# An encoder layer with routed experts: the scatter as 0/1 matrices on gate-scaled rows in two f32r parts, and its steps set between the weight chunks

## The chip, the cores and the metric

One core of a Trainium2 chip runs the kernel. The metric is device time in microseconds (us), median of the runs; 1230.35 us for the kernel before (three runs, 1230.09 to 1231.81).

## The reference, cut to what matters

One layer over 512 tokens of width 1024, all float32: a mixing sub-layer (latent attention beside a convolution), and then a routed mixture of 16 experts, which the change concerns. Each expert takes its best 64 tokens, and its result is scaled by the router's gate and added back to those tokens.

```python
def expert_choice_moe(h, w_router, w_gate, w_up, w_down):
    capacity = CAPACITY_FACTOR * S // N_EXPERTS            # 2 * 512 / 16 = 64
    affinity = jax.nn.softmax(logits, axis=-1)             # logits = h @ w_router
    gates, idx = lax.top_k(affinity.transpose(0, 2, 1), capacity)
    xg = jax.vmap(lambda hb, ib: hb[ib])(h, idx)           # 16 x 64 rows
    a = jnp.einsum('becd,edf->becf', xg, w_gate)           # 1024 -> 2048
    u = jnp.einsum('becd,edf->becf', xg, w_up)
    y = jnp.einsum('becf,efd->becd', jax.nn.silu(a) * u, w_down)
    y = y * gates[..., None].astype(y.dtype)
    return ...                                             # zeros.at[idx].add(y)
# then h = layer_norm(DEEPNORM_ALPHA * h + moe, ln2_g, ln2_b)
```

The weights of one expert are three matrices of 8 MB.

## The kernel before, in words

The mixing sub-layer takes the first 274 us or so and is the same in both kernels. It leaves the normalised tokens in `h1`, the affinities in `aff`, and the rank of every token for experts 0 and 1 in `pos`. Then a loop over the 16 experts follows, written out in Python.

**Weights.** An expert's weights are 24 chunks of 1 MB: 8 of w_gate (k = 0), 8 of w_up (k = 1), 8 of w_down. After the first 22 they come two at a time, 2048 KB to a DMA, into a ring of ten big tiles (`stream`, `take_big`, tile b, L157), all from SP's queue. A DMA into a tile waits until TensorE (PE) has read the tile's former chunks. One tile leaves the ring in expert 1 for the accumulator `acc`, another is lent out in expert 3 for the residual (`residual_pieces`).

**One expert on PE.** For each chunk of gate and up, four matmuls, 128x64 weights by 512 columns, go to the two-bank tiles `gu0` and `gu1` (L1140). The two column halves (partitions 0 to 63 and 64 to 127 of the output) run side by side. Silu on ScalarE (ACT) and a product on VectorE (DVE, L1164) give tile sq; eight transposes (L1185, tile tr) and two copies turn it; then 32 matmuls with w_down go to bank `py` (L1214). Every float32 matmul is two instructions in the trace, so L1140 has 128 and L1214 has 64 instructions an expert.

**Gather.** For a pair of experts (2p, 2p+1) `gather` builds a 0/1 matrix `oh` from the ranks (L1036), multiplies it with `h1` in 32 float32 matmuls (L1044, bank sg), and ACT evacuates to xg (L1045). Then GpSimd (POOL) makes a copy of `oh` with the affinities in place of the ones (`gate`, L1053), PE transposes it (L1056), and ACT writes it to a quarter tile q (L1058). This is the scatter matrix of one expert, with the gates in it.

**Scatter.** ACT copies py to a quarter tile (L1222). In the next expert, eight float32 matmuls (four token blocks t by two halves hf of the width; L1066) multiply the scatter matrix with those rows; hf = 0 uses partitions 0 to 63 and hf = 1 partitions 64 to 127. Each result fills one of two sg banks, and DVE adds it to `acc` (L1072).

**Ranks.** For expert e + 2, within expert e: four transposes (L238, tile tr), comparisons on DVE (L240), and small counting matmuls (L245).

**Order.** The program is written in one order, and a scheduler of the framework then places each instruction on its engine's queue by its own estimate of times. What stands on a queue runs in that order. At the end, `norm_rows` normalises `acc` on DVE and POOL (L1101 to L1106) with gains that ACT spreads from PE transposes (L1013, L1014), and the last expert's own rows are normalised straight from py (L1228 to L1240).

Of the kernel before, what the change touches and what calls it, by code (L numbers as in the profile page):

```python
# [46 lines left out]
def layer_kernel(ctx, tc, x, positions, emb_ln_g, emb_ln_b, w_in, q_norm_g, w_qb, kv_norm_g, w_kvb,  # L47
# [62 lines left out]
    def quarter_tile(q):  # L110
        return slots.tile([128, S], F32, name=f"q{q}")
# [140 lines left out]
    def mask_tile(pool):  # L252
        return pool.tile([128, TT, 128], BF16, name="mask", bufs=4)
# [776 lines left out]
    def gather(pair):  # L1030
        oh = wk.tile([128, TT, 2 * CAP], F32, name="oh", bufs=1)
        xg = wk.tile([128, DC, 2 * CAP], F32, name="xg", bufs=1)
        oh4 = oh.rearrange("p t (e s) -> p t e s", e=2)
        pb = pos[:, :, 2 * pair:2 * pair + 2, None].to_broadcast([128, TT, 2, CAP])
        ib = iota[:, None, None, :].to_broadcast([128, TT, 2, CAP])
        nc.vector.tensor_tensor(oh4, ib, pb, op=OP.is_equal)  # L1036
        width = 1 if pair == 0 else 4
        for c0 in range(0, DC, width):
            p = ps.tile([128, 512], F32, name="sg", bufs=2)
            for c in range(width):  # L1040
                cc = c0 + c
                for t in range(TT):
                    rows = h1[:, t, cc // 2 * 256:cc // 2 * 256 + 256].rearrange("p (n a) -> p a n", a=2)[:, cc % 2]
                    nc.tensor.matmul(p[:, c * 128:(c + 1) * 128], rows, oh[:, t, :], start=t == 0, stop=t == TT - 1)  # L1044
                nc.scalar.activation(xg[:, cc, :], p[:, c * 128:(c + 1) * 128], AF.Identity,  # L1045
                                     scale=gbp[:, 0, cc:cc + 1], bias=gbp[:, 1, cc:cc + 1])
            yield xg

        hot[pair] = oh
        for s in range(1 if pair == E // 2 - 1 else 2):  # L1050
            gate = wk.tile([128, TT, 2, CAP], F32, name="gate", bufs=1)
            ab = aff[:, :, 2 * pair + s, None, None].to_broadcast([128, TT, 2, CAP])
            nc.gpsimd.tensor_tensor(gate, oh4[:, :, s, None, :].to_broadcast([128, TT, 2, CAP]), ab, op=OP.mult)  # L1053
            p = ps.tile([128, 512], F32, name="sg", bufs=2)
            for t in range(TT):
                nc.tensor.transpose(p[:, t * 128:(t + 1) * 128], gate[:, t].rearrange("p a s -> p (a s)"), ident)  # L1056
            g = quarter_tile(s)
            nc.scalar.activation(g, p, AF.Identity)  # L1058
            yield g

    def scatter(y, g, e):
        for t in range(TT):
            pp = []
            for hf in range(2):
                p = ps.tile([128, 512], F32, name="sg", bufs=2)
# [43 lines left out]
    hot = {}  # L1109
    residual = None  # L1110
    pend = None
    nxt = gather(0)
    gT = None
    for e in range(E):
        s = e % 2
        if s == 0:
            if e:
                xg, gT, gate_gen = nxt
        pgu = [ps.tile([128, 2, 512], F32, name=f"gu{k}") for k in range(2)]
        if e:  # L1120
            order = [(k, c) for k in range(2) for c in range(DC)]
        else:

            order = [(k, 2 * j + a) for j in range(DC // 2) for k in range(2) for a in range(2)]
        for k, c in order:
            p = pgu[k]
            if e == 0 and k == 0:
                xg = next(nxt)
            if k == 0 and c == 4 and e + 2 < E:
                pr = ps.tile([128, 512], F32, name="tr")  # L1130
                for t in range(TT):
                    m = mask_tile(wk)
                    compare(e + 2, t, pr[:, t % 2 * 128:(t % 2 + 1) * 128], m)
                    count(t, pr[:, 256:256 + TT], m)
                rank(e + 2, pr[:, 256:256 + TT])
            i = 24 * e + 8 * k + c
            w = w_tiles.pop(i)
            for b in range(2):
                for g in range(2):
                    nc.tensor.matmul(p[g * 64:(g + 1) * 64, b, :], xg[:, c, s * CAP:(s + 1) * CAP], w[2 * b + g],  # L1140
                                     start=c == 0, stop=c == DC - 1)
            if residual is not None and k == 1:
                next(residual, None)
            if c % 2 and not LATE <= i < LATE + 2:

                if (e, k, c) == (1, 1, DC - 1):
                    t4 = take_big(back=False)
                    acc.extend(t4[:, t * D:(t + 1) * D] for t in range(TT))
                elif (e, k, c) == (3, 0, 1):
                    residual = residual_pieces()  # L1150
                    next(residual)
                else:
                    stream(next_chunk[0] + 2)
        sg = pair_tile(F32)
        nc.scalar.activation(sg, pgu[0], AF.Silu)  # L1155
        hh = sg
        last = e == E - 1
        if last:
            gate = last_rows()
        for b in range(2):  # L1160
            if last:
                nc.vector.scalar_tensor_tensor(hh[:, b], sg[:, b], gate, pgu[1][:, b], op0=OP.mult, op1=OP.mult)
            else:
                nc.vector.tensor_tensor(hh[:, b], sg[:, b], pgu[1][:, b], op=OP.mult)  # L1164
        if pend is not None:
            scatter(*pend)
# [7 lines left out]
        if s == 1 and e + 1 < E:  # L1174
            gate_gen = gather((e + 1) // 2)
            for _ in range(DC // 4):
                xg_next = next(gate_gen)
            nxt = xg_next, next(gate_gen), gate_gen
        elif e and not last:
            gT1 = next(gate_gen, None)  # L1180
# [9 lines left out]
        if last:  # L1190
# [16 lines left out]
            nc.scalar.activation(warm, eps2, AF.Sqrt)  # L1207
        for c in range(8):
# [66 lines left out]
```

## Time and profile before

| | us |
|---|---|
| median of 3 runs | 1230.35 |
| the profiled execution | 1228.7 |
| its span, first to last instruction | 1226.9 |
| PE busy | 1147.4 (94%) |
| DVE busy | 409.3 (33%) |
| ACT busy | 237.1 (19%) |
| POOL busy | 213.7 (17%) |

The mean granted clock of TensorE was 0.989. Of the span the chain that ended last gives 81% to PE. Weights are 402.7 MB of the 419.6 MB that are read. A time in the rows below is in us from the span's start; "x16" counts instructions that the view merged; "[0.78 <-DVE b L1072]" is idle time before the first of them, and what ended it.

### The profile page before, as it was taken

To read this page: it belongs to the slowest core of one execution; us is meant where nothing else is said; L and a number is where in the kernel's file an instruction comes from. 1 tells how busy PE (TensorE), PEld (TensorE's weight loads), DVE (VectorE), ACT (ScalarE), POOL (GpSimd) and SP (SyncE) were. 2 spreads that over 40 slices of the span, in tenths; PEclk is the share of its full clock that TensorE was granted. 3 is DMA by queue.
4 is the path that set the end of the run, shared out by engine and by line. 5 is a ranking of instruction groups with operands and counts; after the bars stand their busy time and mean duration, and the time that the engine had idled before them with its cause. 6 is when DMAs were issued, how large, how long until landed. Compare 5 with 4: busy or idle time off the path is not lost.

```text
span 1226.9 us, 13587 instructions
## 1 busy us (share of the span) xinstructions
PE 1147.4 (94%) x5553; PEld 536.4 (44%) x5553; DVE 409.3 (33%) x923; ACT 237.1 (19%) x432; POOL 213.7 (17%) x233
## 2 busy tenths in 40 slices
PE   5898998999999999999999899989999998999996
PEld 4687776774334333432433243324333433344332
DVE  6799898451021116212121202020212021101253
ACT  5445687231111000100100010001000100010020
POOL 6778476210000016000000000000000000000031
PEclk9899999999999999999999999999999999999999
DMA  6430016777999899999999999999999999999981
GB/s 198 131 90 33 1 70 203 279 275 303 406 429 411 369 429 377 430 384 427 427 428 428 428 427 427 427 428 427 427 429 428 427 428 428 428 426 428 428 338 77
DMA packets 43680, 422.84 MB, mean 345 GB/s; under 512 B 5178, under 2 KB 13187, under 8 KB 18018
## 3 DMA queue, kind: packets, MB, share of 16 engines
q1 hardware_dynamic: 42032, 421.28, 83.1%
q8 instruction: 43, 0.70, 0.2%
q10 hardware_dynamic: 1506, 0.43, 0.2%
q0 software_dynamic: 80, 0.26, 0.1%
q14 instruction: 19, 0.16, 0.0%
HBM read 419.60 MB, written 2.36 MB: 344 GB/s over the span
## 4 chain that ended last, share of the span: by engine, by line
PE 81%; DVE 7%; DMA 4%; ACT 3%; issue 3%; POOL 2%; POOLq 0%; SPq 0%; ACTq 0%; DVEq 0%
PE gu L1140 34%; PE py L1214 18%; PE sg L1066 6%; PE sg L1044 6%; PE pj L258 3%; PE pj L259 3%; PE pj L260 3%; PE tr L1185 1%; DVE cv L451 1%; DVE b L1072 1%; DVE mask L240 1%; PE st L773 1%; DMA b<-in_w_down_dram 1%; DMA s<-in_w_in_dram 1%; ACT s L227 1%
## 5 line engine op out<-in xcount | busy, mean ns | idle before, releaser
L1140 PE MATMUL gu<-b,xg 128*64 128x512 f32 x1920 | 436.6, 596 | 0.0
L1140 PEld LDWEIGHTS gu<-b,xg 128*64 128x64 f32 x1920 | 138.9, 137 | 259.3 <-issue 250.7
L1214 PE MATMUL py<-b,sq 128*64 128x512 f32 x976 | 228.3, 609 | 0.0
L1072 DVE TENSOR_TENSOR b<-sg,b 128x512 f32<-128x512 f32 x112 | 73.8, 687 | 201.9 <-PE sg L1066 201.3
L1053 POOL TENSOR_TENSOR gate<-oh,aff 128x512 f32<-128x512 f32 x15 | 16.2, 1077 | 683.3 <-DVE oh L1036 315.7
L1214 PEld LDWEIGHTS py<-b,sq 128*64 128x64 f32 x976 | 66.9, 139 | 122.5 <-issue 117.7
L1066 PE MATMUL sg<-q,q 64*128 64x512 f32 x240 | 88.7, 641 | 16.2 <-DVE b L1072 12.2
L1164 DVE TENSOR_TENSOR sq<-sq,gu 128x512 f32<-128x512 f32 x30 | 19.3, 684 | 231.5 <-PE gu L1140 231.5
L258 PE MATMUL pj<-s,s 128*128 128x512 f32 x189 | 77.8, 420 | 7.6 <-ACT q L433 3.2
L240 DVE SCALAR_TENSOR_TENSOR mask<-tr,aff,ones_b 128x128 bf16<-128x128 f32 x84 | 26.1, 348 | 166.0 <-PE tr L238 166.0
L1044 PEld LDWEIGHTS sg<-oh,h 128*128 128x128 f32 x512 | 64.0, 197 | 31.9 <-issue 24.2
L259 PE MATMUL pj<-s,s 128*128 128x512 f32 x189 | 76.8, 406 | 0.0
L1044 PE MATMUL sg<-oh,h 128*128 128x128 f32 x512 | 71.6, 289 | 3.1 <-ACT xg L1045 2.8
L1045 ACT ACTIVATE xg<-sg,gbp 128x128 f32<-128x128 f32 x64 | 28.7, 457 | 217.4 <-PE sg L1044 124.2
L228 POOL TENSOR_TENSOR s<-s,s 128x512 fp32r<-128x512 f32 (+2 forms) x54 | 64.4, 1216 | 19.6 <-ACT s L227 12.8
L451 DVE SCALAR_TENSOR_TENSOR cv<-s,cw,cv 128x512 f32<-128x512 f32 x83 | 62.2, 750 | 1.7
L260 PE MATMUL pj<-s,s 128*128 128x512 f32 x157 | 62.7, 403 | 0.0
L1066 PEld LDWEIGHTS sg<-q,q 64*128 64x128 f32 x240 | 24.1, 184 | 74.9 <-issue 32.5
L1155 ACT ACTIVATE sq<-gu 128x1024 f32<-128x1024 f32 x16 | 16.4, 1023 | 171.3 <-PE gu L1140 171.3
L1222 ACT ACTIVATE q<-py 128x512 f32<-128x512 f32 x15 | 9.0, 597 | 196.3 <-PE py L1214 196.3
L258 PEld LDWEIGHTS pj<-s,s 128*128 128x128 f32 x189 | 37.4, 199 | 16.8 <-ACT q L433 3.7
L240 DVE SCALAR_TENSOR_TENSOR mask<-tr,aff,before 128x128 bf16<-128x128 f32 x56 | 19.4, 347 | 62.8 <-PE tr L238 62.8
(278 smaller groups left out, 1070.2 us busy)
## 6 DMA issues: line engine op xcount, KB each, us to landing
b<-in_w_down_dram SPq DMA_DIRECT2D x60, 2048.0 KB, 13.6
b<-in_w_gate_dram SPq DMA_DIRECT2D x60, 2048.0 KB, 15.3
b<-in_w_up_dram SPq DMA_DIRECT2D x60, 2048.0 KB, 13.7
s<-in_w_gate_dram SPq DMA_DIRECT2D x8, 1024.0 KB, 6.8
s<-in_w_in_dram SPq DMA_DIRECT2D x12, 512.0 KB, 5.1
s<-in_w_up_dram SPq DMA_DIRECT2D x6, 1024.0 KB, 7.2
s<-in_w_down_dram SPq DMA_DIRECT2D x6, 1024.0 KB, 10.9
s<-in_w_o_dram SPq DMA_DIRECT2D x4, 1024.0 KB, 7.0
```

The lines of the kernel that those rows point to most:

```text
L228: pin(eng, eng.tensor_tensor(lo, src, hi.bitcast(F32), op=OP.subtract))
L240: vector(nc.vector.scalar_tensor_tensor(mask[:, u], here, aff[:, u, e:e + 1], ones_b if u < t else before, op0=OP.is_le, op1=OP.mult, accu ...
L258: tensor(nc.tensor.matmul(p, a[0], b[0], start=start, stop=False, **kw))
L259: tensor(nc.tensor.matmul(p, a[0], b[1], start=False, stop=False, **kw))
L260: tensor(nc.tensor.matmul(p, a[1], b[0], start=False, stop=stop, **kw))
L451: nc.vector.scalar_tensor_tensor(part if k < CW - 1 else cva[j], src[k], w[k], cva[j] if k == n_act else part, op0=OP.mult, op1=OP.add)
L1044: nc.tensor.matmul(p[:, c * 128:(c + 1) * 128], rows, oh[:, t, :], start=t == 0, stop=t == TT - 1)
L1045: nc.scalar.activation(xg[:, cc, :], p[:, c * 128:(c + 1) * 128], AF.Identity, scale=gbp[:, 0, cc:cc + 1], bias=gbp[:, 1, cc:cc + 1])
L1066: nc.tensor.matmul(p, g[hf * 64:(hf + 1) * 64, t * 128:(t + 1) * 128], y[hf * 64:(hf + 1) * 64, :], start=True, stop=True)
L1072: nc.vector.tensor_tensor(a, pp[hf], a, op=OP.add)
L1140: nc.tensor.matmul(p[g * 64:(g + 1) * 64, b, :], xg[:, c, s * CAP:(s + 1) * CAP], w[2 * b + g], start=c == 0, stop=c == DC - 1)
L1214: nc.tensor.matmul(py[hf * 64:(hf + 1) * 64, :], hT2[:, b, j, g * 64:(g + 1) * 64], w[2 * a + hf], start=f == 0 and not last, stop=f == 15)
```

## The change

The scatter matrix keeps its ones: POOL copies `oh` twice side by side (`twice`), PE transposes that, and ACT writes it as f32r (float32 in the form in which a matmul takes one instruction instead of two). The gates come as a column: four float32 matmuls with one column each (L1062) sum `aff` over the chosen tokens. The expert's rows are scaled by that column as they leave py, and split in a rounded part `hi` (ACT, L1070) and the rest `lo` (DVE, L1071), both f32r. The scatter is 16 f32r matmuls instead of 8 float32 ones. `gather` evacuates two chunks to a bank, and `gather`, `ranks` and `scatter` are generators that the loop steps between chunk pairs. The last chunk pair of up runs bank by bank, the second turned bank goes to sg, and the tile for `acc` is taken three chunk pairs earlier.

```diff
+    def choice(pair, s):
+        twice = wk.tile([128, TT, 2, CAP], F32, name="twice", bufs=1)
+        nc.gpsimd.tensor_copy(twice, oh4[:, :, s, None, :].to_broadcast([128, TT, 2, CAP]))
+        both = [twice[:, t].rearrange("p a s -> p (a s)") for t in range(TT)]
         p = ps.tile([128, 512], F32, name="sg", bufs=2)
         for t in range(TT):
+            nc.tensor.transpose(p[:, t * 128:(t + 1) * 128], both[t], ident)
+        g = quarter_tile(s, F32R)
+        nc.scalar.activation(g, p, AF.Identity)
+        p = ps.tile([128, 512], F32, name="sg", bufs=2)
+        for t in range(TT):
+            nc.tensor.matmul(p[:, 0:1], both[t], aff[:, t, 2 * pair + s:2 * pair + s + 1], start=t == 0, stop=t == TT - 1)
+        gate = wk.tile([128, 1], F32, name="gate", bufs=4)
+        nc.vector.tensor_copy(gate, p[:, 0:1])
+        return g, gate
+    def gated(py, gate):
+        hi, lo = quarter_tile(2, F32R), quarter_tile(3, F32R)
+        nc.scalar.activation(hi, py, AF.Identity, scale=gate)
+        nc.vector.scalar_tensor_tensor(lo, py, gate, hi.bitcast(F32), op0=OP.mult, op1=OP.subtract)
+        return hi, lo
-    def scatter(y, g, e):
+    def scatter(parts, g, e):
         for t in range(TT):
-            pp = []
-            for hf in range(2):
-                p = ps.tile([128, 512], F32, name="sg", bufs=2)
-                nc.tensor.matmul(p, g[hf * 64:(hf + 1) * 64, t * 128:(t + 1) * 128], y[hf * 64:(hf + 1) * 64, :],
-                                 start=True, stop=True)
-                pp.append(p)
+            pp = [ps.tile([128, 512], F32, name="sg", bufs=2) for _ in range(2)]
+            for k in range(2):
+                for hf in range(2):
+                    rs = slice(hf * 64, (hf + 1) * 64)
+                    nc.tensor.matmul(pp[hf], g[rs, t * 128:(t + 1) * 128], parts[k][rs, :], start=k == 0, stop=k == 1)
...
+            yield
...
+        for k, j in order:
...
+                if final:
+                    if x == 0:
+                        nc.scalar.activation(sg, pgu[0], AF.Silu)
...
+                elif (k == 0) == last:
+                    if e != 1 or j:
+                        step(sc)
+                else:
+                    step(rk)
...
+        if s == 1 and not last:
+            ga = gather(pair + 1)
         for c in range(8):
...
+            if s == 1 and not last:
+                xg = next(ga)
+        if s == 0:
+            chosen[e] = choice(pair, 0)
+            if e + 2 < E:
+                chosen[e + 1] = choice(pair, 1)
         if not last:
-            if e == 0:
-                gT, gT1 = next(nxt), next(nxt)
-            y = quarter_tile(2 + s)
-            nc.scalar.activation(y, py, AF.Identity)
-            pend = (y, gT1 if s else gT, e)
+            g, gate = chosen.pop(e)
+            rows_of = gated(py, gate), g, e
```

**PE where one expert ends and the next begins.** Line numbers move: L1140 becomes L1170, L1214 becomes L1242, L1066 becomes L1081, L1185 becomes L1211, L1056 becomes L1057. The counts here are matmuls, not instructions. Before, from expert 10 to 11:

```order
L1214 MATMUL py<-b_2524,sq 64x512 x8
L1140 MATMUL gu_4918<-b_2578,xg 64x512 x8
L1066 MATMUL sg<-q_4916,q_4670 128x512 x3
L1140 MATMUL gu_4918<-b_2588,xg 64x512 x8
L1066 MATMUL sg<-q_4916,q_4670 128x512 x2
L1140 MATMUL gu_4918<-b_2610,xg 64x512 x8
L1066 MATMUL sg<-q_4916,q_4670 128x512 x3
```

Now, from expert 6 to 7; q_4164 is `hi`, q_4165 is `lo`:

```order
L1242 MATMUL py<-b_2491,sq 64x512 x8
L1081 MATMUL sg<-q_4164,q_4139 128x512 x2
L1081 MATMUL sg<-q_4165,q_4139 128x512 x2
L1170 MATMUL gu_4168<-b_2501,xg 64x512 x8
L1081 MATMUL sg<-q_4164,q_4139 128x512
L1081 MATMUL sg<-q_4165,q_4139 128x512
L1081 MATMUL sg<-q_4164,q_4139 128x512
L1081 MATMUL sg<-q_4165,q_4139 128x512
L1081 MATMUL sg<-q_4164,q_4139 128x512
L1081 MATMUL sg<-q_4165,q_4139 128x512
L1081 MATMUL sg<-q_4164,q_4139 128x512
L1081 MATMUL sg<-q_4165,q_4139 128x512
```

Block t = 0 now stands right behind py, then a chunk pair, then blocks t = 1 and t = 2 without one between them.

**PE from gu to py in an even expert.** Before, in expert 10:

```order
L1140 MATMUL gu_4724<-b_2666,xg 64x512 x8
L1185 MATMUL tr<-ident,sq 128x128 x8
L1214 MATMUL py<-b_2482,sq 64x512 x8
L238 MATMUL tr<-ident,aff 128x128
L1214 MATMUL py<-b_2492,sq 64x512 x8
```

Now, in expert 6, with the scatter matrix (L1057) and the gate column (L1062) of `choice`:

```order
L1170 MATMUL gu_3941<-b_2607,xg 64x512 x8
L1211 MATMUL tr<-ident,sq 128x128 x4
L1211 MATMUL sg<-ident,sq 128x128 x4
L1057 MATMUL sg<-ident,twice 128x128 x4
L1242 MATMUL py<-b_2642,sq 64x512 x8
L238 MATMUL tr<-ident,aff 128x128
L1062 MATMUL sg<-aff,twice 128x1 x4
```

The eight transposes now fill two banks, and other matmuls stand between them and py.

**DVE at the end of the last expert.** Before (L1101 and L1102 are `norm_rows`, L1228 reads the finished py):

```order
L224 SCALAR_TENSOR_TENSOR mv_5948<-mv_5948 128x1
L1101 SCALAR_TENSOR_TENSOR h_88<-b_2656,mv_5917,b_2492 128x1024
L1101 SCALAR_TENSOR_TENSOR h_88<-b_2656,mv_5927,b_2492 128x1024
L1102 SCALAR_TENSOR_TENSOR h_88<-h_88,mv_5917,b_2492 128x1024
L1102 SCALAR_TENSOR_TENSOR h_88<-h_88,mv_5927,b_2492 128x1024
L1162 SCALAR_TENSOR_TENSOR sq<-sq,gi,gu_5748 128x512 x2
L1187 COPY sq<-tr 128x512
L1228 BN_STATS st_5911<-py 128x6
```

Now (L1115, L1116, L1176, L1213, L1259 are the same steps):

```order
L224 SCALAR_TENSOR_TENSOR mv_6213<-mv_6213 128x1
L1176 SCALAR_TENSOR_TENSOR sq<-sq,gi,gu_6005 128x512 x2
L1213 COPY sq<-sg 128x512
L1115 SCALAR_TENSOR_TENSOR h_88<-b_2586,mv_6182,b_2501 128x1024
L1115 SCALAR_TENSOR_TENSOR h_88<-b_2586,mv_6192,b_2501 128x1024
L1116 SCALAR_TENSOR_TENSOR h_88<-h_88,mv_6182,b_2501 128x1024
L1116 SCALAR_TENSOR_TENSOR h_88<-h_88,mv_6192,b_2501 128x1024
L1259 BN_STATS st_6176<-py 128x6
```

The four wide steps of `norm_rows` moved from ahead of the last product to just ahead of the statistics of py. On PE the 16 transposes of the gains moved with them, from among the last gu chunks to behind L1211: four, then eight matmuls of py, then twelve.

## Rows read from the trace of the kernel before

**Rows 1.** Windows: us, busy of PE, PEld, DVE, ACT, POOL; PEclk, DMA share, GB/s.
```profile
395.00:405.00 10.00, 10.00 (x54) 4.55 (x53) 0.90 (x6) 1.95 (x4) 1.05 (x1) 1.00 0.71 285
525.00:535.00 10.00, 9.72 (x48) 3.40 (x48) 1.21 (x2) 0.60 (x1) 0.00 (x0) 1.00 0.76 288
691.00:751.00 60.00, 58.39 (x294) 24.07 (x290) 9.35 (x24) 6.29 (x12) 1.05 (x1) 1.00 1.01 427
1188.00:1192.00 4.00, 4.00 (x24) 1.67 (x22) 4.00 (x2) 1.57 (x4) 4.00 (x2) 1.00 0.57 227
1192.00:1196.00 4.00, 4.00 (x22) 1.35 (x20) 4.00 (x2) 1.20 (x2) 4.00 (x2) 1.00 0.02 8
```

**Rows 2.** Timeline of SP: first gate tiles of two experts, eight apart.
```profile
593.80 12.86 SPq L157 DMA_DIRECT2D b<-in_w_gate_dram  x4
...
1065.40 12.86 SPq L157 DMA_DIRECT2D b<-in_w_gate_dram  x4
```

**Rows 3.** The line that issues the ring's DMAs.
```profile
DMA to landing us min/median/max: 8.5/14.0/17.9
```

**Rows 4.** Waits of PE, 520 to 1100 us: total, times, longest.
```profile
PE sg L1066 <- DVE b L1072: 11.1, 15, 0.8
PE tr L245 <- DVE mask L240: 9.4, 10, 1.3
PE tr L1185 <- DVE sq L1164: 4.7, 5, 1.2
PE tr L1185 <- ACT sq L1189: 3.7, 5, 0.7
...
PE sg L1066 <- ACT q L1222: 2.2, 5, 0.7
```

**Rows 5.** Timeline of PE in a scatter: start, us, instructions.
```profile
575.96 1.13 PE L1066 MATMUL sg<-q,q 64*128 64x512 f32 x4
577.87 1.12 PE L1066 MATMUL sg<-q,q 64*128 64x512 f32 x2 [0.78 <-DVE b L1072]
578.92 3.65 PE L1140 MATMUL gu<-b,xg 128*64 128x512 f32 x16
```

**Rows 6.** Timeline of PE in f32r matmuls of the input projection.
```profile
225.25 0.39 PE L258 MATMUL pj<-s,s 128*128 128x512 f32 x1
...
228.43 0.39 PE L260 MATMUL pj<-s,s 128*128 128x512 f32 x1
```

**Rows 7.** The chain that ended last: start, us, what.
```profile
490.94 2.08 PE sg L1044 x16
...
1121.42 0.64 PE sg L1084 x13
```

**Rows 8.** Groups by line and form: busy, mean ns.
```profile
L1072 DVE TENSOR_TENSOR b<-sg,b 128x512 f32<-128x512 f32 x112 | 73.8, 687 | 201.9 <-PE sg L1066 201.3
...
L1222 ACT ACTIVATE q<-py 128x512 f32<-128x512 f32 x15 | 9.0, 597 | 196.3 <-PE py L1214 196.3
...
L1238 DVE SCALAR_TENSOR_TENSOR q<-py,mvr,b 128x512 f32<-128x512 f32 x1 | 0.7, 743 | 0.0
```

**Rows 9.** Timeline of PE at the end.
```profile
1190.15 1.09 PE L1013 MATMUL sg<-ident,gb 128*128 128x128 f32 x8
1191.17 10.52 PE L1140 MATMUL gu<-b,xg 128*64 128x512 f32 x48
1202.54 0.75 PE L1185 MATMUL tr<-ident,sq 128*128 128x128 f32 x4 [0.85 <-DVE sq L1162]
...
1204.66 13.95 PE L1214 MATMUL py<-b,sq 128*64 128x512 f32 x64
```

**Rows 10.** Timeline of DVE at the end.
```profile
1187.30 6.79 DVE L1101 SCALAR_TENSOR_TENSOR h<-b,mv,b 128x1024 f32<-128x1024 f32 x2 [4.42 <-DMA b<-in_w_down_dram]
1194.01 6.67 DVE L1102 SCALAR_TENSOR_TENSOR h<-h,mv,b 128x1024 f32<-128x1024 f32 x2
...
1218.66 0.70 DVE L1228 BATCH_NORM_STATS2 st<-py 128x6 f32<-128x512 f32 x1 [13.20 <-PE py L1214]
```

More of the change, by code (lines that the diff above doesn't have):

```diff
@@ new lines, in gated @@
+    def gated(py, gate):
[4 more added lines that the diff above has]
+    def scatter(parts, g, e):
+        for t in range(TT):
+            pp = [ps.tile([128, 512], F32, name="sg", bufs=2) for _ in range(2)]
[3 more added lines that the diff above has]
+                    nc.tensor.matmul(pp[hf], g[rs, t * 128:(t + 1) * 128], parts[k][rs, :], start=k == 0, stop=k == 1)
@@ L1107, in norm_rows, with ranks @@
             nc.sync.dma_start(out[0, t * 128:(t + 1) * 128, :], o)
[L1109 to L1113, printed above, removed]
+    def ranks(e):
+        pr = ps.tile([128, 512], F32, name="tr")
+        ms = []
+        for t in range(TT + 1):
+            if t < TT:
+                ms.append(mask_tile(wk))
+                compare(e, t, pr[:, t % 2 * 128:(t % 2 + 1) * 128], ms[t])
+            if t:
+                count(t - 1, pr[:, 256:256 + TT], ms[t - 1])
+            yield
+        rank(e, pr[:, 256:256 + TT])
@@ L1114, in layer_kernel, with step @@
+    def step(gen):
+        next(gen, None)
+    hot, chosen = {}, {}
+    residual = rows_of = None
+    ga = gather(0)
     for e in range(E):
[L1115 to L1118, printed above, removed]
+        pair, s = divmod(e, 2)
+        last = e == E - 1
         pgu = [ps.tile([128, 2, 512], F32, name=f"gu{k}") for k in range(2)]
         if e:
-            order = [(k, c) for k in range(2) for c in range(DC)]
+            order = [(k, j) for k in range(2) for j in range(DC // 2)]
@@ L1122, in layer_kernel @@
         else:
-            order = [(k, 2 * j + a) for j in range(DC // 2) for k in range(2) for a in range(2)]
-        for k, c in order:
-            p = pgu[k]
[L1127 to L1146, printed above, removed]
+            order = [(k, j) for j in range(DC // 2) for k in range(2)]
@@ new lines, in layer_kernel @@
+        rk = ranks(e + 2) if e + 2 < E else iter(())
+        sg = pair_tile(F32)
+        hh = sg
+        sc = scatter(*rows_of) if e else iter(())
+        if last:
+            gate = last_rows()
+        for k, j in order:
+            p = pgu[k]
+            i = 24 * e + 8 * k + 2 * j
+            ws = [w_tiles.pop(i + a) for a in range(2)]
+            final = k == 1 and j == DC // 2 - 1
+            for x in range(2):
+                for y in range(2):
+                    a, b = (y, x) if final else (x, y)
+                    c = 2 * j + a
+                    if e == 0 and k == 0 and b == 0:
+                        xg = next(ga)
+                    for g in range(2):
+                        nc.tensor.matmul(p[g * 64:(g + 1) * 64, b, :], xg[:, c, s * CAP:(s + 1) * CAP], ws[a][2 * b + g],
+                                         start=c == 0, stop=c == DC - 1)
+                if final:
+                    if x == 0:
+                        nc.scalar.activation(sg, pgu[0], AF.Silu)
+                    if last:
+                        nc.vector.scalar_tensor_tensor(hh[:, x], sg[:, x], gate, p[:, x], op0=OP.mult, op1=OP.mult)
+                    else:
+                        nc.vector.tensor_tensor(hh[:, x], sg[:, x], p[:, x], op=OP.mult)
+                elif (k == 0) == last:
+                    if e != 1 or j:
+                        step(sc)
+                else:
+                    step(rk)
+            if residual is not None:
+                step(residual)
+                step(residual)
+            if not LATE <= i < LATE + 2:
+                if (e, k, j) == (1, 1, 0):
@@ L1157, in layer_kernel @@
[L1157 to L1166, printed above, removed]
+        for _ in range(TT + 1):
+            step(sc)
+            step(rk)
         py = ps.tile([128, 512], F32, name="py")
@@ L1173, in layer_kernel @@
                                      acc[t][:, hf * 512:(hf + 1) * 512], start=t == 0, stop=False)
[L1174 to L1180, printed above, removed]
         hT2 = pair_tile(F32).rearrange("p b (j n) -> p b j n", j=4)
         for b in range(2):
-            p = ps.tile([128, 512], F32, name="tr")
+            p = ps.tile([128, 512], F32, name="sg", bufs=2) if b else ps.tile([128, 512], F32, name="tr")
             for j in range(4):
```

39 lines of the change are left out of this document (14 added, 25 removed).

## The prediction, made before the changed kernel ran

> **What bounds the kernel now.** I read the engine shares first: PE is busy for 94% of the span, and the chain that ended last is PE for 81%. Then I asked whether PE or the stream of weights sets the pace in the expert loop, since the windows show the DMA engines full as well: from 691 to 751 us their share is 1.01 at 427 GB/s [rows 1]. One expert's weights are twelve tiles of 2048 KB, 25.17 MB, which at 427 GB/s take 58.9 us (4.9 us a tile). The pace of the loop, from the first gate tile of one expert to that of the eighth after it, is (1065.40 - 593.80) / 8 = 58.95 us [rows 2]. The two agree, so what decides is who waits. None of PE's waits between 520 and 1100 us is for a DMA; they are for DVE and ACT [rows 4]. A tile lands 14.0 us after its issue in the median [rows 3], that is three tiles in flight out of the nine that circulate, so some five lie loaded and unread. PE is the bound, with the DMA engines saturated just beside it.
>
> The end shows how far PE trails. The last weights have landed by 1192 us (0.57 busy in the 4 us before, 0.02 after) [rows 1]. PE ends the last up chunk, a point I call G, at 1191.17 + 10.52 = 1201.7, and py at 1218.6 [rows 9]. PE is some 27 us behind the weights there. A saving on PE counts until it has eaten this lag; then the weights are the bound. The other reserve is idle DMA time early on, when PE freed tiles too slowly: 285 GB/s from 395 to 405 us and 288 from 525 to 535 [rows 1], each 10 x (1 - 287/427) = 3.3 us.
>
> **The change part by part, for one expert on PE.**
>
> *Scatter, before.* A float32 block, two matmuls on the two partition halves side by side, takes 578.92 - 577.87 = 1.05 us, and a matmul that stands alone takes as long [rows 5]. The order splits eight matmuls into five blocks: 5.25 us.
>
> *Scatter, now.* 16 f32r matmuls, eight steps if the halves still run side by side. An f32r matmul over all 128 partitions takes (228.43 - 225.25) / 14 = 0.227 us [rows 6]. The half-array step is dearer: in py 64 instructions take 13.95 us [rows 9], 0.436 for two side by side, so the two steps of a float32 block would be 0.87, and the block takes 1.05. That is 0.09 more a step. I take 0.32 a step, 2.6 us in all. Bounds: 8 x 0.227 = 1.8 if nothing is added, 16 x 0.32 = 5.1 if the halves run one after the other. I take the value for side by side, since the nearest rows, the same halves of the same tiles, do so.
>
> [...]
>
> *Gate column.* Four float32 matmuls of 128x128 weights and one column, eight instructions. The gather's 16 instructions of 128x128 weights take 2.08 us [rows 7], so 1.04. Lower bound: 64-column weights with two columns take 0.64 for 13, 0.4 for eight [rows 7]. I take 1.04, the same weight size. The transposes (L1057) are those that L1056 had.
>
> *Changes between half-array, column-half and full-array matmuls.* I counted them over PE's order in the expert loop: 311 before, 271 now. 16 instructions ahead of a change take 578.92 to the next block, some 0.1 us more than the 13.95 / 4 = 3.49 without one. 40 x 0.1 / 15 is 0.25 us saved. [...]
>
> *Waits.* Before, the five rows add up to 31.1 us in 9.85 experts, 3.2 an expert [rows 4]. Three kinds shrink: rank counts no longer wait for masks (a chunk of py stands between), and of the waits ahead of py only some 0.4 stays, because the first bank's transposes run while DVE makes the second product. Two grow. Behind py, block 0 waits for `hi` (ACT, 0.60) and then for `lo` (DVE, 0.74 [rows 8]), some 1.2 us after even experts; after odd ones the last gather matmuls lie in it, and 0.6 is left. Blocks 1 and 2 stand together on two sg banks, so block 2 waits for DVE's two adds (0.69 each [rows 8]), 1.4 us; after odd experts this happens twice. Even 0.4 + 1.2 + 1.4 = 3.0, odd 0.4 + 0.6 + 2.8 = 3.8, mean 3.4. I put the difference at nothing, with 1.5 either way.
>
> *Beside PE.* `lo` and the gate copy add 0.9 us to DVE and nothing to POOL, both mostly idle; what they cost PE stands in the waits. SP's DMAs keep their order. `acc` takes its tile three pairs sooner, at a time (expert 1) when the DMA queue is full; its cover gone, it costs up to one tile's spacing, which I leave in the range.
>
> The sum is 5.25 - 2.6 - 1.04 + 0.25 = 1.86 us an expert, 27.9 in 15.
>
> *The tail.* The order puts the 16 gain transposes behind G (1.02 for eight [rows 9], so G comes 2.0 sooner) and the four wide DVE steps with them. From G: the second product and the wait of 0.85 for it [rows 9], transposes to 1.3, four gain transposes to 1.8, eight py matmuls (3.5) to 5.3, four more gain transposes, 0.25 of drain and 0.6 of ACT to 6.6, when the first gain row is whole. The four steps took 1187.30 to 1200.68, 13.4 us, beside POOL [rows 10]; they end at G + 20.0. py ends at about G + 17.8, so its statistics, queued behind those steps, start 2.2 later. From there to the end 1226.9 - 1218.66 = 8.3 [rows 10]. The end is G + 28.3, where it was 1226.9 - 1201.7 = 25.2: 3.1 us lost.
>
> *G.* By PE: 1201.7 - 2.0 - 27.9 = 1171.8. By the weights: of the twelve tiles the last up tile lands four tiles before 1192, at 1172.4, and 16 instructions (3.6) follow: 1176.0, less what the early idle time gives back. At 525 us three scatters (3 x 2.9) less four gate columns (4.2) have put PE 4.5 us ahead, enough for that stretch's 3.3 but not for the one at 400 (one scatter, two columns: 0.8). I take 3.3, between 0 and 6.6: G = 1172.7. The later of the two counts, by a hair the weights: PE is no longer the bound at the end. Span 1172.7 + 28.3 = 1201.0. The profiled execution lies 1.8 above its span and the median of the runs 1.65 above that: 1204.5 us.
>
> **The rivals.**
>
> *PE stays the bound.* The f32r halves run one after another, but with their weight loads hidden: 16 x 0.227 = 3.6, saving 0.86 an expert, G = 1186.8, time 1218.6. Waits that are 1 us longer than mine come to the same. For it: no row shows f32r on half the partitions. Against it: float32 does run side by side.
>
> *The tail hides more.* Bare steps of 0.227, and 6.6 us of idle DMA time given back, so weights end at 1185: G = 1169.4, time 1201; with DVE's wide steps at their lone speed (half) another 2 less: 1199.
>
> *The gain goes into waits.* DVE's adds and `lo` hold PE 1.9 us more an expert than I count, and the saving is nought. With the tail's 3.1 and the 2.0, that is within 0.2% of before. Against it: DVE is 33% busy.
>
> *Slower.* The halves run one after another and each step costs 0.32: 5.1 an expert where 5.25 was, and the gate column on top. The saving is 5.25 - 5.1 - 1.04 + 0.25 = -0.64 an expert, G = 1209.3, time 1241. It decides from the point where the scatter takes over 4.5 us an expert. For it: twice as many matmuls. Against it: they would have to lose an overlap that the same addresses have now.
>
> **How the numbers follow.** The forecast has 0.60, with its own range of 1199 to 1211; PE stays the bound 0.20; the tail hides more 0.07; the gain goes into waits 0.06; slower 0.07. The first three are faster: 0.87. A measurement of this kernel can tell about 0.2% (2.5 us) from no change; within it 0.06, slower 0.07. The range reaches from 1197, under the earliest end of weights, to 1222, over the second case.
>
> **What would show it.** Right: scatter blocks of four f32r matmuls in 0.6 to 0.7 us; gate columns of about 1 us; PE waits of three to four us an expert; DMA share 1.0 from 330 us on, and in the last experts PE waiting for weights; the wide DVE steps after G, and the statistics of py starting right behind them. [...]

## The result and the profile after

The changed kernel takes 1217.61 us, the median of four runs (1214.11 to 1218.25), beside 1230.85 for the kernel before on the same chip: a ratio of 0.9886, 95% interval 0.9866 to 0.9907. It is faster by 13.2 us, where 25.9 were forecast; the time lies inside the stated range of 1197 to 1222. The profiled execution took 1218.25 us, its span 1216.4; it is the slowest of the four.

The first rows are the changed kernel's waits of PE between 520 and 1100 us, which answer to [rows 4].

```profile
PE sg L1081 <- DVE b L1085: 13.8, 18, 0.8
PE gu L1170 <- DVE sq L1178: 8.6, 10, 0.9
PE sg L1081 <- ACT q L1070: 2.5, 3, 0.8
PE tr L245 <- DVE mask L240: 1.3, 1, 1.3
PE sg L1081 <- DVE q L1071: 0.6, 2, 0.3
```

The waits for masks have all but gone, those of the scatter (L1081) for DVE's additions (L1085) have grown, and one is new: the last up matmuls (L1170) wait for DVE's product (L1178). The timeline of PE in an odd expert shows both (start, us, instructions, idle time before them); it answers to [rows 5].

```profile
642.36 0.74 PE L1081 MATMUL sg<-q,q 64*128 64x512 f32 x4
643.88 0.73 PE L1081 MATMUL sg<-q,q 64*128 64x512 f32 x2 [0.78 <-DVE b L1085]
644.53 3.65 PE L1170 MATMUL gu<-b,xg 128*64 128x512 f32 x16
...
670.25 1.94 PE L1170 MATMUL gu<-b,xg 128*64 128x512 f32 x8 [0.86 <-DVE sq L1178]
```

A block of four f32r matmuls takes 644.53 - 643.88 = 0.65 us; 0.64 was forecast. The wait of 0.86 stands in nearly every expert. The new code closes the first up bank before the second, so that DVE can start early; but both banks are one tile, and PE's next write to it waits until DVE has read the first (experiment 2 takes that wait away).

Next, the timeline of SP, the gate tiles of two experts eight apart; it answers to [rows 2].

```profile
598.07 10.63 SPq L157 DMA_DIRECT2D b<-in_w_gate_dram  x4
...
1051.84 10.63 SPq L157 DMA_DIRECT2D b<-in_w_gate_dram  x4
```

The pace is (1051.84 - 598.07) / 8 = 56.72 us an expert, 2.2 less than before and 2.2 under the 58.9 that a DMA stream at 427 GB/s needs. But the first of the two comes 4.3 us later than in [rows 2]. PE runs up to the weights until it waits for one, once and for 0.60 us; the timeline of PE and the chain that ended last both show it:

```profile
1144.74 3.65 PE L1170 MATMUL gu<-b,xg 128*64 128x512 f32 x16 [0.60 <-DMA b<-in_w_gate_dram]
...
1111.66 33.04 DMA b<-in_w_gate_dram
```

Then windows (us, busy of PE, PEld, DVE, ACT, POOL; PEclk, DMA share, GB/s), first of the kernel before, then of the changed one:

```profile
280.00:300.00 20.00, 20.00 (x103) 8.55 (x101) 0.90 (x6) 1.71 (x4) 0.00 (x0) 1.00 0.70 272
460.00:520.00 60.00, 59.49 (x301) 24.72 (x300) 25.25 (x60) 7.62 (x14) 20.76 (x15) 1.00 0.99 403
```

```profile
280.00:300.00 20.00, 20.00 (x102) 8.52 (x101) 2.88 (x19) 1.62 (x5) 0.00 (x0) 1.00 0.60 233
460.00:520.00 60.00, 54.79 (x274) 23.94 (x274) 23.69 (x40) 6.65 (x13) 19.28 (x15) 0.97 0.91 370
...
1196.00:1198.00 2.00, 2.00 (x12) 0.72 (x10) 2.00 (x2) 0.00 (x0) 2.00 (x1) 1.00 0.48 195
1198.00:1200.00 2.00, 2.00 (x12) 0.71 (x10) 2.00 (x2) 0.00 (x0) 2.00 (x2) 1.00 0.01 4
```

The stream lost 20 x (272 - 233) / 427 = 1.8 us more at the loop's start and 60 x (403 - 370) / 427 = 4.6 more from 460 to 520. From 300 to 460 it won 2.0 back (422 GB/s against 417, then 404 against 398), and about 1 us was lost ahead of 280. So the weights have landed by 1198 where it was 1192 [rows 1]: six later, on a stream that is full from 580 us to 1184 (about 428 GB/s). PE and the weights arrive together, both late: the 0.60 us is all that PE waits for them, and in experiment 2 a PE without 11.4 us of its stalls waits for weights instead.

Last the tail: timelines of PE, DVE and POOL, and the chain's last long piece.

```profile
1183.97 1.94 PE L1170 MATMUL gu<-b,xg 128*64 128x512 f32 x8 [0.92 <-DVE sq L1176]
...
1192.78 6.78 DVE L1115 SCALAR_TENSOR_TENSOR h<-b,mv,b 128x1024 f32<-128x1024 f32 x2 [4.54 <-ACT b L1014]
...
1199.48 6.66 DVE L1116 SCALAR_TENSOR_TENSOR h<-h,mv,b 128x1024 f32<-128x1024 f32 x2
...
1206.06 0.69 DVE L1259 BATCH_NORM_STATS2 st<-py 128x6 f32<-128x512 f32 x1
...
1212.38 1.24 POOL L1272 DMA_INDIRECT out_dram<-q,idx  x1 [7.33 <-DMA out_dram<-h]
...
1207.08 4.37 DMA out_dram<-h
```

G is 1185.9. The wide steps start at G + 6.9 and end at G + 20.2, and the statistics of py stand right behind them, as forecast. Then the indirect write waits for the copy of the rows that these steps finished, and starts 2.5 us after its data (1209.13 + 0.75 = 1209.9 on DVE) were ready. The end is G + 30.5.

### The profile page after: what moved, and what is told of

Its sections match the earlier page's. It is cut to its first block, busy times and chain, and to the rows that moved or that the text cites. A ratio compares the mean times of both kernels' runs of the same rounds, so it can differ in the third digit from the quotient of the medians.

```text
span 1216.4 us, 13873 instructions
## 1 busy us (share of the span) xinstructions
PE 1135.0 (93%) x5673; PEld 551.5 (45%) x5673; DVE 425.7 (35%) x953; ACT 238.9 (20%) x432; POOL 206.9 (17%) x233
## 4 chain that ended last, share of the span: by engine, by line
PE 81%; DVE 8%; DMA 6%; ACT 2%; POOL 2%; issue 1%; SPq 0%; POOLq 0%; ACTq 0%; DVEq 0%
PE gu L1170 36%; PE py L1242 17%; PE sg L1044 5%; PE sg L1081 5%; PE pj L258 4%; PE pj L259 3%; PE pj L260 3%; DMA b<-in_w_gate_dram 3%; DVE b L1085 1%; DVE sq L1178 1%; PE st L773 1%; DVE cv L451 1%; PE sg L1062 1%; PE sg L1211 1%; PE tr L238 1%
## 5 line engine op out<-in xcount | busy, mean ns | idle before, releaser
L1170 PE MATMUL gu<-b,xg 128*64 128x512 f32 x1920 | 440.6, 599 | 12.3 <-DVE sq L1178 10.5
L1170 PEld LDWEIGHTS gu<-b,xg 128*64 128x64 f32 x1920 | 134.5, 137 | 280.0 <-issue 252.4
L1242 PE MATMUL py<-b,sq 128*64 128x512 f32 x976 | 223.0, 598 | 0.0
L1053 POOL COPY twice<-oh 128x512 f32<-128x512 f32 x15 | 9.6, 643 | 718.1 <-PE sg L1062 639.8
L1242 PEld LDWEIGHTS py<-b,sq 128*64 128x64 f32 x976 | 68.4, 136 | 111.8 <-issue 103.7
L1085 DVE TENSOR_TENSOR b<-sg,b 128x512 f32<-128x512 f32 x112 | 73.9, 687 | 115.0 <-PE sg L1081 114.6
L1178 DVE TENSOR_TENSOR sq<-sq,gu 128x512 f32<-128x512 f32 x30 | 20.6, 688 | 251.3 <-PE gu L1170 236.2
L1081 PE MATMUL sg<-q,q 64*128 64x512 f32 x240 | 66.9, 459 | 22.8 <-DVE b L1085 19.5
L1081 PEld LDWEIGHTS sg<-q,q 64*128 64x128 f32 x240 | 27.9, 188 | 76.4 <-DVE b L1085 36.6
L1215 ACT ACTIVATE sq<-tr 128x512 f32<-128x512 f32 x16 | 9.6, 597 | 216.5 <-PE tr L1211 113.6
L258 PEld LDWEIGHTS pj<-s,s 128*128 128x128 f32 x189 | 37.6, 200 | 16.7 <-ACT q L433 3.7
L259 PEld LDWEIGHTS pj<-s,s 128*128 128x128 f32 x189 | 37.4, 198 | 7.1
## 6 DMA issues: line engine op xcount, KB each, us to landing
s<-in_w_down_dram SPq DMA_DIRECT2D x6, 1024.0 KB, 11.4
```

What stands on the lines that cost most here:

```text
L258: tensor(nc.tensor.matmul(p, a[0], b[0], start=start, stop=False, **kw))
L259: tensor(nc.tensor.matmul(p, a[0], b[1], start=False, stop=False, **kw))
L1081: nc.tensor.matmul(pp[hf], g[rs, t * 128:(t + 1) * 128], parts[k][rs, :], start=k == 0, stop=k == 1)
L1178: nc.vector.tensor_tensor(hh[:, x], sg[:, x], p[:, x], op=OP.mult)
L1242: nc.tensor.matmul(py[hf * 64:(hf + 1) * 64, :], hT2[:, b, j, g * 64:(g + 1) * 64], w[2 * a + hf], start=f == 0 and not last, stop=f == 15)
```

## The experiments

**1. The residual behind the scatter.** In expert 3 DVE adds scatter and residual in turns, and the residual's additions wait for POOL. The change also steps the residual's pieces in both halves of gate and up, where the kernel before stepped them in the up half alone; the account of the change above does not say so. This run steps them in the up half again.

```diff
-            if residual is not None:
-                step(residual)
-                step(residual)
+            if residual is not None and k == 1 and j > 1:
+                for _ in range(4):
+                    step(residual)
```

> The residual's pieces are stepped in the up half of expert 3 alone, as before the change, so that on VectorE the scatter's additions stand ahead of the residual's. Theory A (the opening lost its gain in expert 3, where scatter and residual meet on VectorE): the scatter's three longest waits there (2.34, 1.35 and 0.44 us) and the 5.11 us block of 16 matmuls go, expert 3 takes about 65 us in place of 68.3, and the time falls by 3 to 5 us, to 1213 to 1215. Theory B (the order is not the cause; the start and the clock are): less than 1 us of change.

1213.15 us (ratio to before 0.9855, 0.9835 to 0.9875): theory A. The interval still touches that of the change (0.9866 to 0.9907); the trace shows where the time went. Expert 3 took 63.5 us in place of 68.3, and the 16 matmuls that had taken 5.11 us, at a granted clock of 0.69 from 470 to 475 us, take 3.65 again. Timelines, first of the changed kernel, then of this one:

```profile
469.45 0.73 PE L1081 MATMUL sg<-q,q 64*128 64x512 f32 x2 [2.34 <-DVE b L1085]
...
471.53 0.90 PE L1081 MATMUL sg<-q,q 64*128 64x512 f32 x2 [1.35 <-DVE b L1085]
472.36 5.11 PE L1170 MATMUL gu<-b,xg 128*64 128x512 f32 x16
...
475.77 4.19 DVE L1028 TENSOR_TENSOR b<-b,b 128x512 f32<-128x512 f32 x1 [3.70 <-POOL b L1026]
```

```profile
468.32 0.73 PE L1081 MATMUL sg<-q,q 64*128 64x512 f32 x2 [1.71 <-DVE b L1085]
468.98 3.65 PE L1170 MATMUL gu<-b,xg 128*64 128x512 f32 x16
```

**2. The up product in two tiles.**

```diff
-        pgu = [ps.tile([128, 2, 512], F32, name=f"gu{k}") for k in range(2)]
+        pg = ps.tile([128, 2, 512], F32, name="gu0")
+        pgu = [[pg[:, b] for b in range(2)], [ps.tile([128, 512], F32, name=f"up{b}") for b in range(2)]]
...
```

> The two banks of the up product become two tiles, so that the last 8 matmuls on the second need not wait until VectorE has read the first (0.86 us in 13 experts, 0.9 in the last). Theory A (weights set the end from 1144 us on, as forecast): TensorE meets the weights some experts earlier and waits for them instead; the weights still land by 1198 in the span, and the time falls by 0 to 2.5 us, to 1215 to 1217.6. Theory B (TensorE still sets the end): all 14 stalls come off, minus 11 to 12 us, 1206.

1215.96 us (0.9883, 0.9866 to 0.9899), 1.7 less than the change, which the intervals cannot tell from none: theory A. The 11.4 us of stalls are gone, and PE waits 7.2 us for weights instead, most of it here:

```profile
PE up L1171 <- DMA b<-in_w_up_dram: 4.6, 4, 1.2
```

**3. The last normalisation earlier.** The spread of the gains and the call of `norm_rows` are moved, unchanged, from behind the transposes of the last expert into its loop:

```diff
+            if last and (k, j) == (1, 0):
+                gb2 = take_big()
...
+                norm_rows()
```

> The spread of the last gains and the normalisation of the finished rows are written ahead of the up half of the last expert. Theory A (the tail was held by VectorE's four wide steps, which end at 1206.1 in the span, and by the copy of the rows to memory behind them): the statistics of the last product follow its end at 1203.9 at once, the indirect copy starts near 1208.4 in place of 1212.4, and the time falls by about 4 us, to 1213.6. Theory B (the wide steps now stand ahead of the last product of gate and up on VectorE): the last product waits for them and the time stays or rises by up to 3 us.

1213.33 us (0.987, 0.9853 to 0.9886): theory A by the time, and by the trace. The last product waited for neither wide step, the statistics start at 1202.45 behind py, the indirect write at 1206.65, and the end is 1210.7 where the change has 1216.4. (The DMA traffic now ends at 1201, the rows' copies and the last weights together, so that the landing of the weights cannot be read from it.) The interval overlaps that of the change; the tail in the trace is what shows the gain.

**4. The scatter in float32, in the new order.**

```diff
...
-        hi, lo = quarter_tile(2, F32R), quarter_tile(3, F32R)
-        nc.scalar.activation(hi, py, AF.Identity, scale=gate)
-        nc.vector.scalar_tensor_tensor(lo, py, gate, hi.bitcast(F32), op0=OP.mult, op1=OP.subtract)
-        return hi, lo
+        y = quarter_tile(2)
+        nc.scalar.activation(y, py, AF.Identity, scale=gate)
+        return y,
...
```

> The scatter in float32 with the scaled rows in one part, in the new order: one part of the change undone. Theory A (the gain is that of the scatter's shorter steps): a step of two matmuls takes 0.52 us again in place of 0.33, the scatter 5.2 us per expert in place of 2.6; 15 experts by 2.6 us, less what its waits for VectorE's additions hid (up to 0.7 us per expert): plus 28 to 39 us, 1245 to 1257. Theory B (the gain came from the new order): less than 10 us more, 1218 to 1228.

1220.76 us (0.9927, 0.9909 to 0.9945), 3.2 behind the change. Theory A falls; B holds. PE's timeline says why:

```profile
641.50 1.13 PE L1079 MATMUL sg<-q,q 64*128 64x512 f32 x4
642.55 3.65 PE L1168 MATMUL gu<-b,xg 128*64 128x512 f32 x16
646.14 1.13 PE L1079 MATMUL sg<-q,q 64*128 64x512 f32 x4
647.20 3.65 PE L1168 MATMUL gu<-b,xg 128*64 128x512 f32 x16
```

Four blocks of 1.05 us, each behind a chunk pair, 4.2 us and in this expert no wait; in f32r two blocks stand together, and the second pays 0.78 for DVE's additions. From 520 to 1100 us the scatter waits 7.0 us for these additions, where the change has 13.8. Gate tiles come every 57.1 us (596.81 to 1053.81 for eight experts), so of the 2.2 us an expert the rest of the change (its order, the 0/1 matrices, the gate columns) brought 1.85 and the f32r parts 0.4.

**5. Experiments 1 to 3 together.**

> The edits of the three runs before together: the residual's pieces in the up half alone, the up product in two tiles, the last gains and row normalisation ahead of the last up half. Alone they measured minus 4.5, minus 1.7 and minus 4.3 us. Theory A (each acts on another stretch: opening, middle, tail): they add up, 1207 us, 1205 to 1209. Theory B (the weights bind from the middle on, and what the opening gives back is lost again): the first two count once, 1210 to 1213.

1208.72 us (0.9823, 0.9796 to 0.985): theory A.

**6 and 7. Spaced blocks**, on top of experiment 5 and alone. The step of the scatter goes to the gate half, once a chunk pair, and each block is pinned behind what PE has in program order. The steps of the ranks go to the up half in exchange:

```diff
-                elif (k == 0) == last:
-                    if e != 1 or j:
+                elif (k == 0) == (e > 1):
+                    if e > 1 and x or e == 1 and j:
                         step(sc)
...
+                    if k == hf == 0:
+                        tc.keep_in_program_order(m)
```

> As the run with the three edits, and each block of four scatter matmuls is pinned behind a chunk pair of the gate half, so that no two blocks stand next to each other and none stands ahead of the first chunk pair. Theory A (the opening is set by TensorE, the rest by the weights): the waits for VectorE's additions and for the first part (1.7 us per expert) and the fall of the granted clock in the 16-matmul burst of expert 4 (0.65 for 10 us) go, but only the idle DMA time of 400 to 580 us comes back: 3 to 5 us less than the three edits, 1202 to 1204. Theory B (TensorE sets the end throughout): 1.7 by 14 and 3.5 more, minus 20 or more. Theory C (it gives nothing, since the weights set all): within 1 us.

> The change with the pinned, spaced scatter blocks alone. Theory A (order and clock in the opening): the burst in expert 4 and the meeting with the residual in expert 3 are spread out, minus 3 to 6 us, 1211.5 to 1214.5. Theory B (the middle counts too): minus 15 us or more, 1202. Theory C (nothing): within 1 us of 1217.6.

On top of experiment 5: 1212.66 us (0.9861, 0.983 to 0.9891), 3.9 more than that experiment, none of the theories; the intervals overlap and the two spans are 1210.5 and 1210.7, so that the run shows neither a gain nor a loss. Alone: 1209.77 us (0.9825, 0.9795 to 0.9855), 7.8 less than the change, more than A. The mechanism is plain in the second run. From 568.8 to 785.1 us PE takes 54.1 us an expert; then it has caught up, and from there to 1021.3 an expert takes 59.0 us, the pace of the stream. Waits of PE between 700 and 1100 us:

```profile
PE gu L1172 <- DMA b<-in_w_up_dram: 17.3, 16, 1.8
PE gu L1172 <- DVE sq L1180: 6.0, 7, 0.9
PE gu L1172 <- DMA b<-in_w_gate_dram: 5.5, 11, 0.6
```

So a faster PE buys nothing behind that point. Alone, the weights land near 1192 and the end is 1209.7. On top of experiment 5 the last weights' DMA is issued 4.5 us later (1173.9 against 1169.4), and the end, with the moved tail, is 1210.5. Both leave the stream idle in expert 3: 363 and 362 GB/s from 460 to 520 us. There the spaced blocks wait for DVE up to 4.1 us, and the granted clock falls (0.86, 0.50 and 0.62 from 465 to 480 us in experiment 7).

**8. The low parts left out.**

```diff
-            for k in range(2):
+            for k in range(1):
...
```

> The change with the low parts of the scaled rows left out of the scatter (the kernel then scatters the high parts alone): TensorE does half of the scatter's steps, 1.3 us per expert less. Theory A (the blocks wait for VectorE's additions, and the weights set the end): the waits take the time, 0 to minus 2 us, 1215.6 to 1217.6. Theory B (the scatter's matmuls set the pace, as the prediction's main term has it): 15 by 1.3, minus 15 to 20 us, 1198 to 1203.

1210.04 us (0.9844, 0.9813 to 0.9875): 7.6 less, between the two. Both fall as they were put: half of the scatter's matmuls gone speeds PE only until it meets the stream (16 us of waits for DMA in the trace), and the weights land six us earlier, by 1192, since the opening gave idle time back: 387 GB/s in place of 370 from 460 to 520 us and 423 in place of 403 from 520 to 580, 5.2 us in sum. The run also prices one step of the scatter; a block is now two f32r matmuls side by side:

```profile
637.46 0.50 PE L1081 MATMUL sg<-q,q 64*128 64x512 f32 x2
637.88 19.11 PE L1170 MATMUL gu<-b,xg 128*64 128x512 f32 x88
```

It takes 0.42 us, and the block of two steps in the change 0.65: the second step adds 0.23.

**9 and 10. The residual in expert 9**, stepped as in experiment 1, alone and with the spaced blocks and the moved tail.

```diff
-                elif (e, k, j) == (3, 0, 0):
+                elif (e, k, j) == (9, 0, 0):
```

> The change with the residual moved from expert 3 to expert 9 and nothing else. Theory A (weights): the opening keeps the DMA busy, the weights land some 5 us earlier, 1211 to 1214. Theory B (TensorE): its 8 us are lost in expert 9 in place of expert 3, 1216 to 1219.

> The spaced scatter, the last gains and row normalisation ahead of the last up half, and the residual moved from expert 3 to expert 9. Theory A (the end is the landing of the last weights plus a tail, 18.3 us behind it with the change's tail and 12 with the moved one; the landing is set by the idle DMA time before 580 us; the residual can stand where TensorE waits for weights anyway): of the spaced run's idle time at 460 to 520 us (share 0.88 of 60 us) 5 to 7 us come back, the weights land by 1185 to 1187 and the time is 1198 to 1201. Theory B (the residual costs TensorE the same 8 to 10 us wherever it stands, and a buffer is missing from the ring): 1203 to 1209.

Alone: 1206.26 us (0.9813, 0.9784 to 0.9842), below A's range. 3.6 us between the two profiles are not the edit's: this one's loop starts at 277.0, the change's at 280.7. Part of the gain is experiment 1's, whose stepping it shares: its span is 8.3 us under that of experiment 1, 3.1 of them the earlier start. With both: 1200.47 us (0.9755, 0.9736 to 0.9774): theory A. The window that lost the stream is full in it, and the DMA traffic, weights and the rows' copies, ends near 1187:

```profile
460.00:520.00 60.00, 59.03 (x310) 24.53 (x308) 11.65 (x35) 7.00 (x12) 0.46 (x1) 1.00 1.01 428
...
1184.00:1186.00 2.00, 2.00 (x13) 0.58 (x9) 0.00 (x0) 0.00 (x0) 0.00 (x0) 1.00 0.39 158
1186.00:1188.00 2.00, 2.00 (x12) 0.71 (x10) 0.00 (x0) 0.00 (x0) 0.00 (x0) 1.00 0.08 31
```

**11. The same with the scatter of experiment 4.**

> As the run with the spaced scatter, the moved tail and the residual in expert 9, but with the scatter in float32, the scaled rows in one part. Theory A (the weights set the pace of 58.9 us per expert, and TensorE needs 54 with the parts and 56 to 57 with float32, both below it): within 2 us of the run in two parts, apart from the opening's share. Theory B (the parts are what lets TensorE keep up): 10 us or more behind it.

1215.44 us (0.9866, 0.9838 to 0.9894), 15 behind. B by the number, A by the middle: from 741.8 to 969.7 us PE takes 57.0 us an expert, less than the stream, and meets it behind that, with 7.8 us of waits in all. But of the 13.7 us between the two spans 4.8 lie in the start of the loop, which is not the edit's, and 8.2 in experts 1 and 2, which took 110.4 us in place of 102.2. There the timeline of PE shows the two halves of a block apart from each other, so that nothing runs beside a float32 matmul:

```profile
409.06 1.12 PE L1079 MATMUL sg<-q,q 64*128 64x512 f32 x2
410.11 2.79 PE L1170 MATMUL gu<-b,xg 128*64 128x512 f32 x10
```

Eight such matmuls, 1.05 us each, stand in expert 2: 8.4 us of scatter, where the f32r blocks of experiment 10 take 3.5. In expert 1 it is 4.4 against 2.8. That is 6.5 of the 8.2; so the parts count where PE is the bound, in the opening, and here much of their price is the order again.

**12. One wide row of DVE behind the last product.** In experiment 10's kernel the last product waited 3.7 us for the wide steps.

```diff
-                norm_rows()
+                norm_rows((2, 3, 0))
...
+            norm_rows((1,))
```

Row 1's first step is pinned behind the copy of the product's transpose.

> As the run with the spaced scatter, the moved tail and the residual in expert 9, but of VectorE's two rows of the last normalisation one stands ahead of the last product of gate and up and the other behind its copy, so that the product need not wait (3.7 us in the run before). Theory A (TensorE's last work set the end there): the 3.7 us come off, 1196 to 1198. Theory B (the last weights, landed by 1186 in the span, set it with the product of the last chunk, 3.65 us, and 8.5 us of statistics and writing behind it): 1 to 2 us, 1198.5 to 1199.5.

1198.12 us (0.9766, 0.9747 to 0.9786). The wait for the wide steps is gone (0.85 for the product's first half is left, as in the change), and the time lies between the two ranges, 0.1 us above A's; by its ratio it cannot be told from experiment 10's kernel (0.9755). Both beat the kernel before, and with 0.977 and 0.976 against 0.989 the change as well.

## Why the prediction was right in kind and short by half

The sum missed by G: 1185.9 where 1172.7 stood, 13.2 us more, and the tail added 2.2. That is 15.4 in the span; the median is 13.1 above its forecast, since the profiled run is the slowest of the four. The rival "PE stays the bound" had 1218.6, next to the 1217.6 measured, but by luck: its halves one after another, or waits 1 us longer, did not come. The weights, which the forecast had landed by 1192 at the latest, landed by 1198.

*What held.* The halves of an f32r block run side by side (0.65 against 0.64). The size was right, the reason given for it was not: a block is 0.20 longer than two full-array steps of 0.227 [rows 6], but by experiment 8 that comes once a block (0.42 for one step) and not as 0.09 with each step. The second step, on the same partitions as the first, adds only 0.23. What the 0.20 is, no run takes apart. The 0.1 us ahead of a change of matmul form is in both traces: 16 instructions ahead of a scatter block take 3.58 before (578.92 to 582.50) and 3.59 now (644.53 to 648.12), against 3.49. What makes it, and what 40 changes fewer brought, no run shows: the 0.25 was an estimate. The gate column cost 0.81 an expert against 1.04. From expert 5's start (572.4 before, 580.3 after) to G the kernel gained 23.7 us, 2.0 of it the gain transposes: 1.97 an expert against 1.86. PE did catch up with the weights, by a hair, and experiments 2, 6 and 7 show that the stream is the bound once PE is any faster.

*What held only in sum.* The scatter fell from 5.25 to 2.6 as forecast, and the waits are 26.8 us in the stretch of [rows 4], where the forecast summed 31.1: the new 0.86 an expert, where I let 0.4 stand, and 0.78 for each block that stands behind another, where I counted 1.4. Experiment 4 shows that most of what was gained an expert (1.85 of 2.2) needs no f32r at all: blocks that are not split cost 4.2 in float32 and wait less, and the forecast put the whole difference on the parts.

*The step that failed* is that of the idle time: "At 525 us three scatters (3 x 2.9) less four gate columns (4.2) have put PE 4.5 us ahead", and "I take 3.3, between 0 and 6.6". The same step stands in PE's own sum, which takes 1.86 off each of 15 experts, the first four with them. PE was not ahead there but behind: the loop started 2.2 us later (a difference of the run, in code that is the same; other profiles differ by more), and experts 1 to 4 lost 5.7 us where 7.4 were to be gained. With the 1.2 gained behind them these give 2.2 + 13.1 - 1.2 = 14.1, the way from PE's forecast 1171.8 to 1185.9. The 13.1 are 4.0 in experts 1 and 2 together, 2.9 in expert 3 and 6.3 in expert 4. Experiment 1 takes 4.8 back in expert 3, where the order puts scatter and residual on DVE in turns. In expert 4 the scatter stands in one burst, and the expert takes 60.5 us where it was 56.1 before and is 52.0 with spaced blocks. The granted clock fell in the burst, in windows of the changed kernel:

```profile
520.00:525.00 5.00, 4.85 (x27) 1.62 (x25) 1.41 (x6) 0.41 (x1) 0.00 (x0) 1.00 0.99 423
525.00:530.00 5.00, 4.38 (x11) 2.46 (x12) 3.73 (x6) 0.00 (x0) 0.00 (x0) 0.65 1.02 436
530.00:535.00 5.00, 5.00 (x17) 1.44 (x17) 1.38 (x2) 0.00 (x0) 0.00 (x0) 0.66 0.77 324
```

Over experts 1 to 4 PE's waits are 9.0 us where they were 5.3, and the clock cost some 5.2 us where it was 1.7 (an estimate: each window of 5 us times what its granted clock lacks of 1). These are 7.2 of the 13.1; the rest stays open, most of it in experts 1 and 2, which no run takes apart, nor the earlier tile for `acc`. So the stream did not get its 3.3 us back; it lost 6 more, and a stream that is full from there on lands that much later. The bound of that term, "between 0 and 6.6", left out a loss, though the order in which the two kinds of additions alternate could be read beforehand.

*The tail* came as worked out up to the end of the wide steps. Its 0.25 of drain can be read from [rows 9]: four transposes take 0.75 and follow each other within 0.51 (1.02 for eight). The forecast counted the 8.3 us from there on as before, and missed that the indirect write comes behind the rows' copies on the output: 1216.4 - 1206.06 = 10.3. Experiment 3 takes that chain away.

## What to carry to other kernels

When two bounds lie close together (here the forecast had G at 1171.8 by PE and 1172.7 by the weights), ask what a saving does to the stream's idle time: a stream that is full to the end can only be helped where it is not full, in the opening. Side work that shares an engine with the pacing loop (here the residual) belongs where that loop waits anyway. And before paying for faster matmuls, look at where the blocks stand, so that none waits for its own buffers. In the order of the change the f32r parts brought 3.2 us, and spacing their blocks 7.8 more (experiments 4 and 7); with experiment 11's halves apart the parts were worth some 9 (13.7 less the 4.8 of the start).

## What the hardware showed

A wide DVE step of 128x1024 takes 3.4 us beside POOL's and 1.28 alone. Timelines of DVE and POOL in the kernel of experiment 12: first beside POOL, then started 0.11 us ahead of POOL's, last without wide work on POOL:

```profile
1157.38 3.48 DVE L1119 SCALAR_TENSOR_TENSOR h<-b,mv,b 128x1024 f32<-128x1024 f32 x1 [1.61 <-ACT b L1014]
1157.42 5.66 POOL L1123 TENSOR_TENSOR h<-h,b 128x1024 f32<-128x1024 f32 x2 [1.85 <-ACT b L1014]
1163.13 1.28 DVE L1120 SCALAR_TENSOR_TENSOR h<-h,mv,b 128x1024 f32<-128x1024 f32 x1 [2.27 <-ACT b L1014]
1163.24 5.70 POOL L1124 TENSOR_TENSOR h<-h,b 128x1024 f32<-128x1024 f32 x2 [0.16 <-ACT b L1014]
...
1174.41 1.28 DVE L1119 SCALAR_TENSOR_TENSOR h<-b,mv,b 128x1024 f32<-128x1024 f32 x1
```

The lone step is 2.7 times as fast as the one beside POOL (1.28 against 3.48), and not twice, as the prediction's "half" has it, a guess for which no row stood. The step that started 0.11 us ahead of POOL's took 1.28, the one that started 0.04 ahead 3.48; what makes the difference, no run shows.

The clock fell in the burst of expert 4. The timeline of PE in the changed kernel:

```profile
519.85 3.65 PE L1170 MATMUL gu<-b,xg 128*64 128x512 f32 x16
...
524.12 0.73 PE L1081 MATMUL sg<-q,q 64*128 64x512 f32 x3
525.43 5.40 PE L1081 MATMUL sg<-q,q 64*128 64x512 f32 x12 [0.58 <-DVE b L1085]
```

On half the array, three blocks with DVE's additions between them, the twelve matmuls took 5.40 us; at full clock it would be some 3.5, an estimate from 0.65 for a block and 0.78 for a wait. The granted clock of 0.65 is a mean: windows of 0.25 us show 1.00 up to 526.50 us and 0.50 from 526.75 to 533.25, as in these two:

```profile
526.00:526.25 0.25, 0.25 (x2) 0.23 (x2) 0.06 (x1) 0.00 (x0) 0.00 (x0) 1.00 0.62 262
526.75:527.00 0.25, 0.15 (x2) 0.07 (x1) 0.25 (x2) 0.00 (x0) 0.00 (x0) 0.50 1.23 524
```

It is 1.00 again from 533.5 us on. In experiment 4, whose blocks are spaced, 520 to 580 us show 1.00, but spacing alone does not keep the clock up: in that run it fell at 485 to 495 us (0.80 and 0.86), and in experiment 7 in expert 3, both behind waits for DVE. The start of the expert loop, behind the same code in all kernels, lies between 275.5 and 280.9 us in the profiles: two kernels' stretches can be compared to tenths of a us, the ends of two profiles only to some 5.
